# Choosing the byte offset of the weights' halves in SBUF by their use as stationary or moving operand

## The chip, the cores and the metric

The kernel runs on one core of one Trainium2 chip. The metric is the device time of one execution in microseconds (us); TensorE is called PE, VectorE DVE, ScalarE ACT, GpSimd POOL and SyncE SP, as in the profile.

## What is computed

A decoder trunk of two layers over one sequence of 256 tokens with 2048 channels, in float32. Layer 0 is attention with a forget gate (16 heads of 128), layer 1 a causal convolution module (31 taps per channel). Each has one input projection, a SiLU gate and one output projection; an RMS norm stands before each and at the end.

```python
def fox_mixer(h, w_in, b_f, w_out):          # layer 0
    q, k, v, gate, f_logit = split(h @ w_in)  # 2048 x (4*2048 + 16)
    c = cumsum(log_sigmoid(f_logit + b_f))
    s = q k^T * 128**-0.5 + c[:, None] - c[None, :]   # causal, per head
    return (softmax(s) @ v * silu(gate)) @ w_out

def conv_mixer(h, w_in, b_in, dw, dw_b, ln_g, ln_b, w_out):   # layer 1
    a, b, gate = split(h @ w_in + b_in)       # 2048 x (3*2048)
    u = conv31(a * sigmoid(b), dw) + dw_b     # causal, per channel
    return (silu(layernorm(u)) * silu(gate)) @ w_out
```

## The kernel before

**Matrices in two halves.** PE multiplies float32r numbers here. Each float32 weight or activation is therefore split into a high half (an ACT copy, `hi`, L100) and a low half (the rest, `lo`, a subtraction on DVE or POOL, L101), and each product is made of three matmuls: high by high, high by low, low by high. A weight tile is 1 MB (128 partitions by 2048 floats): SP loads it (`raw`, L112), ACT and DVE or POOL split it, PE uses it. Each of the pools `rawp`, `hip` and `lop` has three slots; ACT writes a `hi` slot when PE has finished the tile three before it.

**Two forms of projection.** `products_t` (L216) gives a transposed result. The weights' 128 columns are the stationary operand (`w[:, nt * P : ...]`), the 256 tokens of one activation tile are the moving one. One weight tile feeds 48 such matmuls. It makes q, k and the gate of layer 0, layer 0's output projection, and the whole input projection of layer 1. `products_n` (L244 to L246) gives a result by rows. There 128 tokens of the activations are stationary and 512 (in the last part 256) weight columns move. It makes v of layer 0 (`pv`) and layer 1's output projection (`po`). In the trace a matmul's row reads result<-moving,stationary.

**Where the tiles lie.** The pool `big` holds the activations: `ah`, `al` (input of layer 0, later of layer 1's first blocks), `yh`, `yl` (output of the attention), `nh`, `nl` (normed input of layer 1), `y1b` (second half of layer 1's branch output) and `xt` (halves of one late weight tile). The first half of the branch output, `ya` (in the trace `y1a`), lies in the pool `ph2`. The built kernel places all tiles of `big` and all slots of `rawp`, `hip` and `lop` at addresses that leave remainder 160 when divided by 256, since each is a multiple of 256 bytes long (16384, 8448 and 8192). Each operand is taken at a multiple of 512 bytes from its tile's start, so it keeps that remainder. `ph2` starts at 160 too, but ahead of `ya` in it lies `dwT` with 1984 bytes, 64 short of a multiple of 256, so `ya` is at remainder 96.

**Stages and order.** Layer 0 goes by four groups of heads: k, q, gate, v, and the attention of a group is put between the next group's matmuls by an agenda that counts matmul steps (`at`, `step`). PE's order is the written one throughout. From the last part of layer 0's output projection on (`all_order`), DVE, ACT and POOL run in the written order too. In layer 1 the convolution is done by DVE, one instruction for each tap and channel tile (`tap`, L824), put into PE's steps by `put` and `pump`. When a pair of channel tiles is done, ACT takes it out (`pair_end`, L876 and L877), POOL adds it to the sums for the layer norm (L880, L881, L884), and both do so in line with their share of the weights' split. After the last pair, PE adds up the rows (`column_sums`, L724, `pstat`), DVE and POOL make mean and scale (L966 to L975), and `gated` and `gated2` make `ya` and `yb` (`y1b` in the trace).

Of the kernel before, what the change touches and what calls it, by code (L numbers as in the profile page):

```python
# [8 lines left out]
F32 = mybir.dt.float32  # L9
F32R = mybir.dt.float32r  # L10
# [3 lines left out]
P = 128  # L14
D = 2048
S = 256
# [12 lines left out]
RMS_EPS = 1e-6  # L29
LN_EPS = 1e-5  # L30
LN_ROWS = 6


@with_exitstack
def tile_hybrid_trunk(
# [20 lines left out]
    const = ctx.enter_context(tc.tile_pool(name="const", bufs=1))  # L56
    big = ctx.enter_context(tc.tile_pool(name="big", bufs=1))
    rawp = ctx.enter_context(tc.tile_pool(name="rawp", bufs=3))
    hip = ctx.enter_context(tc.tile_pool(name="hip", bufs=3))
    lop = ctx.enter_context(tc.tile_pool(name="lop", bufs=3))  # L60
# [5 lines left out]
    ph = part.enter_context(tc.tile_pool(name="ph1", bufs=2))  # L66
# [5 lines left out]
    w_fin = fox_w_in[0].rearrange("(kt p) n -> p kt n", p=P)  # L72
    w_fout = fox_w_out[0].rearrange("(kt p) n -> p kt n", p=P)
    w_cin = conv_w_in[0].rearrange("(kt p) n -> p kt n", p=P)
    w_cout = conv_w_out[0].rearrange("(kt p) n -> p kt n", p=P)
# [17 lines left out]
    def load_x(c0, c1):  # L93
        nc.sync.dma_start(xn[:, :, c0:c1], xv[:, :, c0:c1])

    n_stream = [0]
    ctx.enter_context(tc.manual_schedule(engines={mybir.EngineType.PE}))

# [4 lines left out]
    def weight_tile(wv, c0, width, g, pieces=1, pool=None):  # L103

        kg = 2048 // width
        i = n_stream[0]
        n_stream[0] += 1
        raw = rawp.tile([P, 4 * NARROW], F32, tag="raw", name=f"raw{i}")[:, 0:2048]
        rv = raw.rearrange("p (k n) -> p k n", k=kg)
        kp = kg // pieces  # L110
        for q in range(pieces):
            nc.sync.dma_start(  # L112
                rv[:, q * kp : (q + 1) * kp], wv[:, g * kg + q * kp : g * kg + (q + 1) * kp, c0 : c0 + width]
            )
        return raw

    def split_tile(raw, width, lo_engs, hi=None, lo=None):

        kg = 2048 // width
        i = n_stream[0]  # L120
        n_stream[0] += 1
        if hi is None:
            hi = hip.tile([P, 2048], F32R, tag="hi", name=f"hi{i}")
            lo = lop.tile([P, 2048], F32R, tag="lo", name=f"lo{i}")
        pc = 2048 // len(lo_engs)
        for q, eng in enumerate(lo_engs):
            cs = slice(q * pc, (q + 1) * pc)
            split(hi[:, cs], lo[:, cs], raw[:, cs], eng)
        return hi.rearrange("p (k n) -> p k n", k=kg), lo.rearrange("p (k n) -> p k n", k=kg)

    def stream(wv, c0, width, lo_engs, pieces=1, ahead=False, made=(), order=None):

        kg = 2048 // width
        order = order or range(KT // kg)
        made = list(made)
        for g in range(KT // kg):
            while len(made) < (KT // kg if ahead else g + 1):
                i = len(made)
                raw = weight_tile(wv, c0, width, order[i])
                made.append(split_tile(raw, width, (lo_engs[i % len(lo_engs)],) * pieces))  # L140
            hv, lv = made[g]
            for kk in range(kg):
                yield g * kg + kk, hv[:, kk, :], lv[:, kk, :]


    feed = {"specs": [], "made": []}

    def feed_tiles(wv, c0, width, engs, order=None):

        n = KT * width // 2048  # L150
        first = len(feed["specs"])
        feed["specs"] += [(wv, c0, width, (order or range(n))[g], engs) for g in range(n)]
        return first

    def feed_make(upto):
        while len(feed["made"]) <= min(upto, len(feed["specs"]) - 1):
            wv, c0, width, g, engs = feed["specs"][len(feed["made"])]
            feed["made"].append(split_tile(weight_tile(wv, c0, width, g), width, engs))

    def fed(first, width):  # L160
        kg = 2048 // width
        for g in range(KT // kg):
            feed_make(first + g + 2)
            hv, lv = feed["made"][first + g]
            feed["made"][first + g] = None
            for kk in range(kg):
                yield g * kg + kk, hv[:, kk, :], lv[:, kk, :]
# [129 lines left out]
    with tc.manual_schedule(engines={mybir.EngineType.Activation, mybir.EngineType.DVE, mybir.EngineType.SP}):  # L297
# [40 lines left out]
        def k_split(kt):  # L338
            split_act(kt, 0, ah, al, pts[kt // 2][:, (kt % 2) * S : (kt % 2 + 1) * S])
            g, kk = kt // 4, kt % 4  # L340
            if kk == 0:
                his.append(hip.tile([P, 2048], F32R, tag="hi", name=f"hik{g}"))
                los.append(lop.tile([P, 2048], F32R, tag="lo", name=f"lok{g}"))
            cs = slice(kk * 512, (kk + 1) * 512)
            split(his[g][:, cs], los[g][:, cs], raws[g][:, cs], nc.gpsimd if kt % 2 and kt < KT - 1 else nc.vector)

# [101 lines left out]
    def gate_and_forget(c0):  # L448

        fw = ph.tile([P, KT, 2 * H], F32R, tag="v0", name="fw", bufs=1)  # L450
        ps = banks_t(512)

        pf = bank("pf")[0 : 2 * H, 0:S]
        for g in range(4):
            i = n_stream[0]
            n_stream[0] += 1
            raw = rawp.tile([P, 4 * NARROW], F32, tag="raw", name=f"raw{i}").rearrange("p (k n) -> p k n", k=4)
            nc.sync.dma_start(raw, w_fin[:, 4 * g : 4 * g + 4, c0 : c0 + NARROW])
            hi = hip.tile([P, 2048], F32R, tag="hi", name=f"hi{i}").rearrange("p (k n) -> p k n", k=4)
            lo = lop.tile([P, 2048], F32R, tag="lo", name=f"lo{i}").rearrange("p (k n) -> p k n", k=4)  # L460
            split(hi, lo, raw[:, :, 0:512], nc.vector)
            fg = fw[:, 4 * g : 4 * g + 4, :]
            split(fg[:, :, 0:H], fg[:, :, H : 2 * H], raw[:, :, 512:NARROW], nc.vector)
            for kk in range(4):
                kt = 4 * g + kk
                products_t(ps, kt, hi[:, kk, :], lo[:, kk, :], tiles(ah), tiles(al), range(4))
                if kk == 3:
                    for k in range(4 * g, kt + 1):
                        nc.tensor.matmul(pf, fw[:, k, :], ah[:, k, :], start=(k == 0), stop=False)
                        nc.tensor.matmul(pf, fw[:, k, :], al[:, k, :], start=False, stop=(k == KT - 1))  # L470
        zt = ph.tile([P, S], F32, tag="yy", name="zt")[0 : 2 * H]
        nc.vector.tensor_tensor(zt, pf, rb[0 : 2 * H, 0, :], op=ALU.mult)
        nc.vector.tensor_scalar(zt, zt, bf[0 : 2 * H], None, op0=ALU.add)
        at(2, lambda: forget_gates(zt))
        return ps
# [141 lines left out]
    for pos, hg in enumerate(ORDER):  # L617
# [38 lines left out]
            ph.tile([P, 512], dt, tag=f"v{i}", name=f"v{i}_{hg}", bufs=1) for i, dt in enumerate((F32R, F32R, F32))  # L656
        ]
        ps = [psj.tile([P, 512], F32, tag="pj", name=f"pv{hg}_{m}") for m in range(2)]
        for kt, hv, lv in stream(w_fin, 2 * D + hg * 512, 512, VE):
            for m in range(2):  # L660
                products_n(ps[m], kt, hv, lv, tiles(ah), tiles(al), m, kt == 0, kt == KT - 1)
        nc.scalar.activation(vN[0], ps[0], AF.Copy, scale=r0[:, 0:1])
# [22 lines left out]
        a_first[c0] = feed_tiles(w_cin, c0, width, GE if c0 == P else engs)  # L685
    for c in range(4):
        g_first[c] = feed_tiles(w_cin, 2 * D + c * 512, 512, GE)
    cout0 = feed_tiles(w_cout, 0, 512, VE * 2)

    def residual_add(n, b, ps):  # L690
        kp = slice(4 * n + 2 * b, 4 * n + 2 * b + 2)
# [24 lines left out]
        for b in range(2):  # L716
            residual_add(n, b, ps)

    rb1 = const.tile([P, 1, S], F32, name="rb1")

    def column_sums(ps, c0, src, last=True):

        for m in range(2):
# [21 lines left out]
    part.close()  # L745
    ph = ctx.enter_context(tc.tile_pool(name="ph2", bufs=2, reuse_waits="tile"))
    psa = ctx.enter_context(tc.tile_pool(name="psa2", bufs=3, space=bass.MemoryType.PSUM, reuse_waits="tile"))

    def kept_bank(name):

# [235 lines left out]


    HK = KT // 2
    ya = ph.tile([P, 2, HK, S], F32R, name="y1a", bufs=1)
    gts = {}  # L990

    def gated(cp):
# [99 lines left out]
        at(14 + 1.5 * i, lambda i=i: residual_rows(i // 2, i % 2))  # L1092
    for n in range(3):
        ps = [psj.tile([P, 512], F32, tag="pj", name=f"po{n}_{m}") for m in range(2)]
        for kt, hv, lv in fed(cout0, 512) if n == 0 else stream(w_cout, n * 512, 512, VE, 4):
            for m in range(2):
                products_n(ps[m], kt, hv, lv, yh, yl, m, kt == 0, kt == KT - 1)
        if n == 0:
            all_order.close()
        for m in range(2):  # L1100
            cs = slice(n * 512, (n + 1) * 512)
            nc.vector.tensor_tensor(o[:, m, cs], ps[m], o[:, m, cs], op=ALU.add)
            junk = ph.tile([P, 512], F32, tag="ev", name=f"junk{n}_{m}", bufs=4)
            nc.scalar.activation(junk, o[:, m, cs], AF.Square, accum_out=ssn[:, m, n : n + 1])
            nc.gpsimd.tensor_tensor(o[:, m, cs], o[:, m, cs], fgb[:, cs], op=ALU.mult)

    wt = []
    for g in range(4):
        raw = weight_tile(w_cout, 3 * 512, 512, g)
        if g == 0:  # L1110
            wt.append(split_tile(raw, 512, VE, xt[:, 0, :], xt[:, 1, :]))
        else:
            wt.append(split_tile(raw, 512, VE))
    for m in range(2):
        for c0, c1 in ((1536, 1792), (1792, 2048)):
            ps = psj.tile([P, 512], F32, tag="pj", name=f"po{c0}_{m}")
# [41 lines left out]
```

## Time and profile before

| | us |
|---|---|
| median of three runs | 886.54 (884.74 to 886.8) |
| the profiled execution, its time | 885.23 |
| the profiled execution, its span | 883.4 |
| PE busy | 871.9 |
| DVE busy | 569.4 |
| ACT busy | 420.6 |
| POOL busy | 363.4 |

The profile is of one execution. The span runs from the first to the last instruction; 1.8 us of the time lie around it. Matmuls overlap, so a row's mean duration is longer than the distance to the next one; the rate is read from starts in the timeline.

### The profile page before, as it was taken

What the parts mean: (1) busy time and instruction counts of PE and PEld (TensorE: products, weight loads), DVE (VectorE), ACT (ScalarE), POOL (GpSimd) and SP (SyncE); (2) the same over time, 40 slices, a digit from 0 to 9 for tenths busy, and PEclk for the clock granted to TensorE, in tenths of its full rate; (3) what the DMA queues carried; (4) which work ended last, traced back from release to release, by engine and by line L of the source; (5) the groups of instructions that cost most, each with busy time, mean ns of one, the idle gap of its engine ahead of it and who ended that gap; (6) DMA issues with size and microseconds to landing.
All of it is one profiled execution on the core that took longest, in us unless ns stands there. A gap on an engine that the chain in (4) does not pass through costs nothing.

```text
span 883.4 us, 15933 instructions
## 1 busy us (share of the span) xinstructions
PE 871.9 (99%) x6652; PEld 842.4 (95%) x6652; DVE 569.4 (64%) x1043; ACT 420.6 (48%) x558; POOL 363.4 (41%) x229
## 2 busy tenths in 40 slices
PE   9999999999999999999999999999999999999996
PEld 9999889989999899989999999999999999998896
DVE  5765456445544454446555679999999994567641
ACT  5753344345534454346544474344443455657531
POOL 4131955103410142102200068888998898521110
PEclk9999999999999999999999999999999999999998
DMA  9878988886567998965455565555555555556522
GB/s 299 222 205 189 179 155 144 165 194 174 143 185 179 173 173 153 184 190 189 135 174 178 147 191 192 191 169 193 179 179 188 162 187 189 179 191 238 180 107 96
DMA packets 99500, 157.71 MB, mean 179 GB/s; under 512 B 2676, under 2 KB 40676, under 8 KB 99300
## 3 DMA queue, kind: packets, MB, share of 16 engines
q1 hardware_dynamic: 99092, 155.63, 65.2%
q8 instruction: 52, 0.85, 0.4%
q10 hardware_dynamic: 336, 1.07, 0.3%
q14 instruction: 20, 0.16, 0.1%
HBM read 154.59 MB, written 2.10 MB: 177 GB/s over the span
## 4 chain that ended last, share of the span: by engine, by line
PE 95%; issue 1%; DMA 1%; ACT 1%; POOL 1%; DVE 0%; SPq 0%; POOLq 0%; DVEq 0%
PE pt L216 72%; PE pv L244 3%; PE pv L245 3%; PE pv L246 3%; PE po L246 3%; PE po L244 3%; PE po L245 3%; DMA rawk<-in_fox_w_in_dram 1%; PE sc L564 1%; PE ptr L593 1%; PE po L609 1%; ACT hi L100 0%; PE sc L565 0%; PE po L610 0%; PE hr L1086 0%
## 5 line engine op out<-in xcount | busy, mean ns | idle before, releaser
L100 ACT ACTIVATE hi<-raw 128x2048 fp32r<-128x2048 f32 (+2 forms) x185 | 270.6, 1486 | 303.9 <-PE pt L216 210.3
L101 DVE TENSOR_TENSOR lo<-raw,hi 128x2048 fp32r<-128x2048 f32 (+2 forms) x140 | 221.4, 1607 | 187.6 <-ACT hi L100 187.3
L101 POOL TENSOR_TENSOR lo<-raw,hi 128x2048 fp32r<-128x2048 f32 x45 | 208.1, 4641 | 42.7 <-ACT hi L100 42.7
L216 PE MATMUL pt<-ah,hi 128*128 128x256 f32 x768 | 219.6, 286 | 0.0
L216 PE MATMUL pt<-ah,lo 128*128 128x256 f32 x768 | 217.3, 283 | 0.0
L216 PE MATMUL pt<-al,hi 128*128 128x256 f32 x768 | 217.3, 283 | 0.0
L216 PE MATMUL pt<-nh,hi 128*128 128x256 f32 x704 | 199.6, 283 | 0.0
L216 PE MATMUL pt<-nh,lo 128*128 128x256 f32 x704 | 199.3, 283 | 0.0
L216 PE MATMUL pt<-nl,hi 128*128 128x256 f32 x704 | 199.2, 283 | 0.0
L824 DVE SCALAR_TENSOR_TENSOR acc<-u,dwT,acc 128x256 f32<-128x256 f32 x478 | 188.3, 472 | 0.0
L216 PEld LDWEIGHTS pt<-al,hi 128*128 128x128 f32 x768 | 147.4, 192 | 0.1
L216 PEld LDWEIGHTS pt<-ah,hi 128*128 128x128 f32 x768 | 147.3, 192 | 0.1
L216 PEld LDWEIGHTS pt<-ah,lo 128*128 128x128 f32 x768 | 147.3, 192 | 0.0
L216 PEld LDWEIGHTS pt<-nl,hi 128*128 128x128 f32 x704 | 135.1, 192 | 0.0
L216 PEld LDWEIGHTS pt<-nh,hi 128*128 128x128 f32 x704 | 135.1, 192 | 0.0
L216 PEld LDWEIGHTS pt<-nh,lo 128*128 128x128 f32 x704 | 135.1, 192 | 0.0
L216 PE MATMUL pt<-yh,hi 128*128 128x256 f32 x256 | 73.3, 286 | 0.0
L216 PE MATMUL pt<-yl,hi 128*128 128x256 f32 x256 | 72.5, 283 | 0.6 <-POOL yl L101 0.6
L216 PE MATMUL pt<-yh,lo 128*128 128x256 f32 x256 | 72.4, 283 | 0.0
L558 POOL CAST la<-ones 64x256 fp32r<-64x256 f32 x16 | 8.0, 500 | 134.9 <-PE sc L567 134.7
L244 PE MATMUL pv<-hi,ah 128*128 128x512 f32 x128 | 50.0, 390 | 0.0
L216 PEld LDWEIGHTS pt<-yl,hi 128*128 128x128 f32 x256 | 49.1, 192 | 0.8 <-POOL yl L101 0.8
(260 smaller groups left out, 1219.0 us busy)
## 6 DMA issues: line engine op xcount, KB each, us to landing
raw<-in_fox_w_in_dram SPq DMA_DIRECT2D x56, 1024.0 KB, 7.4
raw<-in_conv_w_in_dram SPq DMA_DIRECT2D x48, 1024.0 KB, 5.2
raw<-in_fox_w_out_dram SPq DMA_DIRECT2D x16, 1024.0 KB, 5.1
raw<-in_conv_w_out_dram SPq DMA_DIRECT2D x16, 1024.0 KB, 5.3
raw<-in_fox_w_in_dram SPq DMA_DIRECT2D x4, 1056.0 KB, 11.1
rawk<-in_fox_w_in_dram SPq DMA_DIRECT2D x4, 512.0 KB, 10.4
xn<-in_x_dram SPq DMA_DIRECT2D x3, 512.0 KB, 10.7
rawk<-in_fox_w_in_dram SPq DMA_DIRECT2D x4, 256.0 KB, 5.8
```

Source lines behind the costliest of these rows:

```text
L100: nc.scalar.activation(dst_hi, src, AF.Copy)
L101: lo_eng.tensor_tensor(dst_lo, src, dst_hi.bitcast(F32), op=ALU.subtract)
L216: nc.tensor.matmul(ps[nt // 2][:, (nt % 2) * S : (nt % 2 + 1) * S], w[:, nt * P : (nt + 1) * P], a(kt), start=(kt == 0 and i == 0 and nt % ...
L244: nc.tensor.matmul(ps, ah(kt)[:, ms], hv, start=first, stop=False)
L245: nc.tensor.matmul(ps, al(kt)[:, ms], hv, start=False, stop=False)
L246: nc.tensor.matmul(ps, ah(kt)[:, ms], lv, start=False, stop=last)
L558: nc.gpsimd.tensor_copy(la[0:64], ones[0:64, 0:1].broadcast_to([64, S]))
L564: nc.tensor.matmul(sc[:, 0:S], qT[q][:, j, :], kT[k][:, j, :], start=(i == 0), stop=False)
L593: nc.tensor.transpose(out=pt[:, dst * P : (dst + 1) * P], in_=p[:, srcs * P : (srcs + 1) * P], identity=ident)
L609: nc.tensor.matmul(po[:, 0:S], vN[v][:, js], pts[p], start=(i == 0), stop=False)
L824: nc.vector.scalar_tensor_tensor(acc, src, w, acc, op0=ALU.mult, op1=ALU.add)
```

## The change

Every slot of `hip` and `lop` becomes 64 floats (256 bytes) longer, and the halves begin in it at an offset. Where the weights are stationary it is 48 floats (192 bytes), which makes remainder 96. Where they move with 512 columns it is 0 (remainder 160), and where they move with 256 columns in the last part it is 16 floats (64 bytes, remainder 224). `ya` gets 16 floats of offset (remainder 160 in place of 96). To make room, `rb1` (1024 bytes) moves from the pool `const` to the start of `ph2`, which changes no remainder. `xt` stays at 160. No instruction is added, removed or put elsewhere.

```diff
+SLACK = 64
+AS_STATIONARY = 48
+AS_MOVING = 0
+AS_MOVING_256 = 16
...
+    def half_tile(pool, tag, name, off):
+        return pool.tile([P, 2048 + SLACK], F32R, tag=tag, name=name)[:, off : off + 2048]
...
-    def split_tile(raw, width, lo_engs, hi=None, lo=None):
+    def split_tile(raw, width, lo_engs, hi=None, lo=None, off=AS_STATIONARY):
...
-            hi = hip.tile([P, 2048], F32R, tag="hi", name=f"hi{i}")
-            lo = lop.tile([P, 2048], F32R, tag="lo", name=f"lo{i}")
+            hi = half_tile(hip, "hi", f"hi{i}", off)
+            lo = half_tile(lop, "lo", f"lo{i}", off)
...
-        for kt, hv, lv in stream(w_fin, 2 * D + hg * 512, 512, VE):
+        for kt, hv, lv in stream(w_fin, 2 * D + hg * 512, 512, VE, off=AS_MOVING):
...
-    cout0 = feed_tiles(w_cout, 0, 512, VE * 2)
+    cout0 = feed_tiles(w_cout, 0, 512, VE * 2, off=AS_MOVING)
...
-    rb1 = const.tile([P, 1, S], F32, name="rb1")
...
+    rb1 = ph.tile([P, 1, S], F32, name="rb1", bufs=1)
...
-    ya = ph.tile([P, 2, HK, S], F32R, name="y1a", bufs=1)
+    ya = ph.tile([P, 2 * HK * S + SLACK], F32R, name="y1a", bufs=1)[:, 16 : 16 + 2 * HK * S]
+    ya = ya.rearrange("p (i k t) -> p i k t", i=2, k=HK)
...
-        for kt, hv, lv in fed(cout0, 512) if n == 0 else stream(w_cout, n * 512, 512, VE, 4):
+        for kt, hv, lv in fed(cout0, 512) if n == 0 else stream(w_cout, n * 512, 512, VE, 4, off=AS_MOVING):
...
-            wt.append(split_tile(raw, 512, VE))
+            wt.append(split_tile(raw, 512, VE, off=AS_MOVING_256))
```

The tiles of the first k projection (`hik`, `lok`) and of the gate with the forget columns get `AS_STATIONARY` in the same way.

## Rows read from the trace of the kernel before

**Rows 1.** The page: busy time by engine; shares of the closing chain.

```profile
PE 871.9 (99%) x6652; PEld 842.4 (95%) x6652; DVE 569.4 (64%) x1043; ACT 420.6 (48%) x558; POOL 363.4 (41%) x229
...
PE 95%; issue 1%; DMA 1%; ACT 1%; POOL 1%; DVE 0%; SPq 0%; POOLq 0%; DVEq 0%
```

**Rows 2.** The chain in order of time: start us, length us, what.

```profile
545.06 197.26 PE pt L216 x1644
```

**Rows 3.** PE's groups by form: shapes, count | busy us, mean ns | idle.

```profile
L216 PE MATMUL pt<-ah,hi 128*128 128x256 f32 x768 | 219.6, 286 | 0.0
...
L216 PE MATMUL pt<-nh,hi 128*128 128x256 f32 x704 | 199.6, 283 | 0.0
...
L246 PE MATMUL po<-lo,y1a 128*128 128x512 f32 x48 | 18.8, 392 | 0.0
L246 PE MATMUL po<-lo,y1b 128*128 128x512 f32 x48 | 18.7, 390 | 0.0
...
L246 PE MATMUL po<-lo,y1b 128*128 128x256 f32 x32 | 9.0, 283 | 0.0
...
L246 PE MATMUL po<-lo,y1a 128*128 128x256 f32 x16 | 4.4, 277 | 0.0
```

**Rows 4.** Timeline of PE, first of the last four passes: start us, us.

```profile
852.54 0.28 PE L246 MATMUL po<-xt,y1a 128*128 128x256 f32 x1
...
855.01 0.28 PE L246 MATMUL po<-lo,y1a 128*128 128x256 f32 x1
...
856.08 0.28 PE L246 MATMUL po<-lo,y1b 128*128 128x256 f32 x1
...
857.88 0.28 PE L246 MATMUL po<-lo,y1b 128*128 128x256 f32 x1
```

**Rows 5.** The same timeline, second of the last four passes.

```profile
858.68 0.28 PE L246 MATMUL po<-xt,y1a 128*128 128x256 f32 x1
...
861.06 0.28 PE L246 MATMUL po<-lo,y1a 128*128 128x256 f32 x1
```

**Rows 6.** The same timeline, stationary `y1a` under 512 columns, later `y1b`.

```profile
783.70 0.39 PE L245 MATMUL po<-hi,y1a 128*128 128x512 f32 x1
...
785.99 0.39 PE L246 MATMUL po<-lo,y1a 128*128 128x512 f32 x1
...
840.98 0.39 PE L244 MATMUL po<-hi,y1b 128*128 128x512 f32 x1
...
841.66 0.39 PE L244 MATMUL po<-hi,y1b 128*128 128x512 f32 x1
```

**Rows 7.** PE's waits: us in total, times, longest us.

```profile
PE sc L566 <- POOL la L559: 2.2, 1, 2.2
```

**Rows 8.** The convolution's window: busy us (count) by engine, clock, DMA share, GB/s.

```profile
526.90:742.10 215.20, 215.15 (x1792) 214.93 (x1791) 208.53 (x542) 95.85 (x96) 189.04 (x52) 1.00 0.56 182
```

**Rows 9.** Timeline of ACT and POOL after the fifth and sixth pairs' taps.

```profile
683.97 0.51 ACT L876 ACTIVATE dall<-acc,par 128x256 f32<-128x256 f32 x1 [3.83 <-DVE acc L824]
...
694.67 18.47 POOL L101 TENSOR_TENSOR lo<-raw,hi 128x2048 fp32r<-128x2048 f32 x4
...
716.95 13.88 POOL L101 TENSOR_TENSOR lo<-raw,hi 128x2048 fp32r<-128x2048 f32 x3
```

**Rows 10.** Timeline of PE: first use of those tiles' `lo`, and the row sums.

```profile
700.64 0.28 PE L216 MATMUL pt<-nh,lo 128*128 128x256 f32 x1
...
723.68 0.28 PE L216 MATMUL pt<-nh,lo 128*128 128x256 f32 x1
...
742.53 0.58 PE L724 MATMUL pstat<-ones,accs 128*128 128x1 f32 x4
```

**Rows 11.** Timeline of DVE: its wait for the row sums.

```profile
743.15 0.16 DVE L966 TENSOR_SCALAR mean<-pstat 128x2 f32<-128x2 f32 x1 [4.58 <-PE pstat L724]
```

**Rows 12.** Timeline of POOL and PE: the gate's last weight tile.

```profile
773.18 4.63 POOL L101 TENSOR_TENSOR lo<-raw,hi 128x2048 fp32r<-128x2048 f32 x1 [6.06 <-ACT hi L100]
...
777.89 0.36 PE L216 MATMUL pt<-nh,lo 128*128 128x256 f32 x1
```

More of the change, by code (lines that the diff above doesn't have):

```diff
@@ L129, in split_tile, with stream @@
         return hi.rearrange("p (k n) -> p k n", k=kg), lo.rearrange("p (k n) -> p k n", k=kg)
-    def stream(wv, c0, width, lo_engs, pieces=1, ahead=False, made=(), order=None):
+    def stream(wv, c0, width, lo_engs, pieces=1, ahead=False, made=(), order=None, off=AS_STATIONARY):
         kg = 2048 // width
@@ L139, in stream @@
                 raw = weight_tile(wv, c0, width, order[i])
-                made.append(split_tile(raw, width, (lo_engs[i % len(lo_engs)],) * pieces))
+                made.append(split_tile(raw, width, (lo_engs[i % len(lo_engs)],) * pieces, off=off))
             hv, lv = made[g]
@@ L146, in tile_hybrid_trunk, with feed_tiles @@
     feed = {"specs": [], "made": []}
-    def feed_tiles(wv, c0, width, engs, order=None):
+    def feed_tiles(wv, c0, width, engs, order=None, off=AS_STATIONARY):
         n = KT * width // 2048
         first = len(feed["specs"])
-        feed["specs"] += [(wv, c0, width, (order or range(n))[g], engs) for g in range(n)]
+        feed["specs"] += [(wv, c0, width, (order or range(n))[g], engs, off) for g in range(n)]
         return first
@@ L156, in feed_make @@
         while len(feed["made"]) <= min(upto, len(feed["specs"]) - 1):
-            wv, c0, width, g, engs = feed["specs"][len(feed["made"])]
-            feed["made"].append(split_tile(weight_tile(wv, c0, width, g), width, engs))
+            wv, c0, width, g, engs, off = feed["specs"][len(feed["made"])]
+            feed["made"].append(split_tile(weight_tile(wv, c0, width, g), width, engs, off=off))
     def fed(first, width):
@@ L341, in k_split @@
             if kk == 0:
-                his.append(hip.tile([P, 2048], F32R, tag="hi", name=f"hik{g}"))
-                los.append(lop.tile([P, 2048], F32R, tag="lo", name=f"lok{g}"))
+                his.append(half_tile(hip, "hi", f"hik{g}", AS_STATIONARY))
+                los.append(half_tile(lop, "lo", f"lok{g}", AS_STATIONARY))
             cs = slice(kk * 512, (kk + 1) * 512)
@@ L458, in gate_and_forget @@
             nc.sync.dma_start(raw, w_fin[:, 4 * g : 4 * g + 4, c0 : c0 + NARROW])
-            hi = hip.tile([P, 2048], F32R, tag="hi", name=f"hi{i}").rearrange("p (k n) -> p k n", k=4)
-            lo = lop.tile([P, 2048], F32R, tag="lo", name=f"lo{i}").rearrange("p (k n) -> p k n", k=4)
+            hi = half_tile(hip, "hi", f"hi{i}", AS_STATIONARY).rearrange("p (k n) -> p k n", k=4)
+            lo = half_tile(lop, "lo", f"lo{i}", AS_STATIONARY).rearrange("p (k n) -> p k n", k=4)
             split(hi, lo, raw[:, :, 0:512], nc.vector)
```

## The prediction

> **What bounds the kernel now.** I read the busy times and the closing chain first. PE is busy 99% of the span and makes up 95% of the chain [rows 1]. The chain in order of time then gives the rate: one piece of it is 1644 matmuls of L216 in 197.26 us, 120.0 ns from one to the next, with no break [rows 2]. So the end is set by PE's rate, and within it by L216, the form with 256 moving columns. There are 768 of each of its three products with `ah`/`al` and 704 with `nh`/`nl` [rows 3]; by the code another 256 with `yh`/`yl` and 64 in the first k projection. That is 3 x 1792 = 5376 matmuls, or 645 us at 120.0 ns.
>
> The question is then whether 120.0 ns is the least that such a matmul takes. The kernel before holds its own experiment. In the four last passes, 256 columns move over weights at remainder 160, and the stationary operand is first `y1a` (remainder 96, 64 below the moving one), then `y1b` (160, the same). In the second pass 21 steps with `y1a` take 861.06 - 858.68 = 2.38 us, 113.3 ns each [rows 5]; the third and the fourth repeat this. In the first pass the 21 steps take 2.47 us, 117.6 ns each, and 15 steps with `y1b` take 1.80 us, 120.0 ns each [rows 4]. The mean durations show the same: 277 ns with `y1a`, 283 ns with `y1b`, and 283 to 286 in L216, whose two operands are both at 160 [rows 3]. Matmul, form, stage and moving tiles are alike, so the address of the stationary operand makes the difference.
>
> With 512 moving columns it goes the other way, a little: 10 steps with `y1a` take 2.29 us (229 ns), 3 with `y1b` 0.68 us (227 ns) [rows 6]; the means are 392 and 390 ns [rows 3].
>
> [...]
>
> **What is saved per matmul.** The three good passes save 6.7 ns each (120.0 - 113.3), the first 2.4 ns [rows 4, 5]. I can't tell what sets the first apart: ACT and DVE were at work during it and hardly in the others, but it may also be the phase in which the stream began. I take the mean of the four passes, (2.4 + 3 x 6.7) / 4 = 5.6 ns, and keep 2.4 and 6.7 as the ends.
>
> **Layer 0.** Here 2880 L216 matmuls (704 x 3 with `ah`/`al`, since 64 of each 768 belong to layer 1's first blocks, and 256 x 3 with `yh`/`yl`) save 2880 x 5.6 = 16.1 us. The feed keeps up: a tile of 48 matmuls takes 5.8 us now and 5.5 us then, and DVE, ACT and POOL have work for 64%, 48% and 41% of the span [rows 1]. The 192 matmuls of the first k projection are worth 1.1 us at most and nothing at least, since they follow the first loads; I take 0.5. Against that stands PE's one long wait, 2.2 us for POOL's part of the first head [rows 7]. POOL's forget gate runs at its own speed there, so the some 80 matmuls ahead of that wait give nothing: -0.5 us. Sum: **16.1 us**, between 6.7 and 19.9.
>
> **Layer 1, the convolution.** This stage will not give its full share. From 526.9 to 742.1 us PE is busy for 215.15 of 215.20 us, but DVE for 208.53 [rows 8], with taps that no offset makes shorter. Most of DVE's free time is one piece of 4.58 us at the end, when it waits for the row sums [rows 11]. PE at 5.6 ns less for each of some 1790 matmuls would come 10 us early and find DVE not ready. Three places hold it back; "lead" is how much earlier than now PE passes, beyond what the whole stage gains by starting earlier.
> - After the fifth pair's taps, ACT takes the pair out (it waited 3.83 us for DVE), and the weights' split and POOL's sums queue behind that. POOL then makes four `lo` tiles without a break from 694.67 on, the first of them done at 694.67 + 18.47 / 4 = 699.3, and PE reads it at 700.64 [rows 9, 10]. The lead there is at most 1.3 us.
> - After the sixth pair the same: `lo` is done at 716.95 + 13.88 / 3 = 721.6, PE reads it at 723.68 [rows 9, 10]. From the first place to here 192 matmuls bring 1.1 us, so the lead would be 2.4; the cap is 2.1.
> - At the row sums (742.53 [rows 10]) another 157 matmuls have brought 0.9 us: lead 3.0, below the 4.58 us that DVE waits there now.
>
> Ahead of the convolution, some 70 matmuls (0.4 us) count, between the output projection and the row sums that start DVE's chain. Behind the row sums there are some 340 matmuls up to the output projection, 1.9 us. Part of it goes, because the norm and gating work of DVE and ACT runs at its own speed: the gate's last `lo` tile, queued behind it, is done at 773.18 + 4.63 = 777.81 and read at 777.89 [rows 12]. I take 1.2. Sum for the stage: 0.4 + 3.0 + 1.2 = **4.6 us**, where its 2304 matmuls at the full rate would have given 13. The rest becomes short waits of PE for POOL and ACT in the gate chunks.
>
> **Output projection.** The two splits that write at a shifted address are taken at no cost: the kernel writes `y1a` at 96 and `y1b` at 160 already, inside work that PE hides. Under 512 columns `pv` stays at equal remainders, and 144 matmuls with `ya` move from 229 to 227 ns: 0.3 us. Under 256 columns `ya` over the later weight tiles stays 64 below (160 and 224), 96 matmuls with `y1b` now come 64 below: 0.5 us. The 48 with `xt`, both at 160 then, lose 0.3 us. Sum: **0.5 us**.
>
> **Total.** 16.1 + 4.6 + 0.5 = 21.2 us from the profiled 885.23 gives 864.0. That execution is 1.3 us below the median of 886.54 and inside the runs' 884.74 to 886.8, so I say **864.5**.
>
> **Rivals.**
> - **A, the weak phase.** If L216 runs as the first pass did, at 117.6 ns, perhaps because other engines are at work nearly always: layer 0 gives 6.7, the convolution and the gate some 3 (the lead is 1.3 at the first cap, and less is added), the end 0.3, in all 10 us: **875**. For it: that pass was the one with other engines busy. Against it: the steps of 229 ns under 512 columns hold with those engines at work, so their work needn't matter.
> - **B, the convolution follows.** If the three caps are not binding, because POOL and DVE have more room than I read, 5376 x 5.6 = 30 us: **855**. Against it stands DVE's 208.53 of 215.20 us.
> - **C, nothing changes.** If the difference belongs to the quiet end of the kernel or to `y1a` itself and not to the distance of 64 bytes, L216 stays at 120.0 ns: **886**. Against it: `y1b` ran at 120.0 ns in the same passes.
> - **D, slower.** Under 512 columns the distance of 64 costs 2 to 2.5 ns where equal remainders are best. If a stream whose weights are stationary behaves like that one, since the stationary tile changes between `hi` and `lo` and the moving one between `ah` and `al`, 5376 x 2.4 = 13 us are added, PE being the bound: **898**. It decides as soon as L216's step is over 120.0 ns.
>
> **How the numbers follow.** The forecast (858 to 870) has 0.63, A 0.17, B 0.07, C 0.06, D 0.07. The range reaches from the best case of the forecast to A. At 6.7 ns layer 0 gives 19.9, the row sums the full 4.6, 2.7 around them and 0.7 at the end, 27.9 us in all: 857 from the profiled time. At 2.4 ns it is 10 us, 876.5 from the median, so 877. That leaves about 0.2 outside. What a measurement here can tell from no change is about 0.3%, 2.7 us. Faster by more: forecast, A and B, 0.87. Within: C, 0.06. Slower by more: D, 0.07.
>
> **What would show it.** The step between starts of L216 at 113 to 118 ns in layer 0, and the mean duration near 277 ns; `pv` unchanged at 227 ns; `y1b` in the last passes at 113 and `xt` over `ya` back at 120. In the convolution, DVE's wait for the row sums shrinks from 4.58 us, its busy share of that window goes to 98% or more, and PE shows new waits for POOL's `lo` or DVE's `u` between 670 and 725 us. The page should show PE idle there although it is the faster engine. Wrong would be: L216 at 120 ns or more (C, D), no new waits in the gate chunks (B), or a wait long enough that the granted clock, 1.00 in this window [rows 8], falls behind it; that would cost little while DVE sets the pace.

## The result, and the profile after

The changed kernel takes 875.96 us (median of 4 runs, 875.0 to 876.41), the kernel before 886.01 us beside it (4 runs, 884.74 to 886.8): a ratio of 0.9885, 95% interval 0.9873 to 0.9897. It is faster, by 10.1 us. The forecast was 864.5, a gain of 22. The time is inside the range and within 1 us of rival A.

The profiled execution took 876.26 us (span 874.4). Line numbers of the kernel after are 6 to 10 higher: L216 is now L225. The page, busy time by engine and the closing chain (to compare with [rows 1]):

```profile
PE 861.1 (98%) x6652; PEld 831.4 (95%) x6652; DVE 569.7 (65%) x1043; ACT 420.5 (48%) x558; POOL 363.6 (42%) x229
...
PE 90%; DVE 3%; POOL 3%; issue 2%; ACT 1%; POOLq 0%; DVEq 0%
```

PE lost 10.8 us of busy time, and the other engines did what they did before. DVE and POOL, hardly in the chain before, now make up 3% of it each. The chain in order of time, start and length in us, shows the step, that is the time from one matmul's start to the next one's:

```profile
332.32 43.81 PE pt L225 x372
425.37 75.76 PE pt L225 x641
538.38 135.69 PE pt L225 x1152
692.75 41.18 PE pt L225 x346
```

The first piece has 372 matmuls in 43.81 us, 117.8 ns each; the third has 1152 in 135.69, again 117.8. (The second opens behind a wait of 0.70 us with a slower first matmul, 0.22 us to the next start; from its second start on the step is 117.8 too.) Before, it was 120.0 [rows 2]. So the saving is 2.2 ns a matmul, not 5.6. The groups by form (shapes, count | busy us, mean ns | idle) say the same:

```profile
L225 PE MATMUL pt<-ah,hi 128*128 128x256 f32 x768 | 216.8, 282 | 0.0
...
L225 PE MATMUL pt<-nh,hi 128*128 128x256 f32 x704 | 196.8, 280 | 0.0
...
L255 PE MATMUL po<-lo,y1a 128*128 128x512 f32 x48 | 18.7, 391 | 0.0
L255 PE MATMUL po<-lo,y1b 128*128 128x512 f32 x48 | 18.7, 390 | 0.0
L255 PE MATMUL po<-lo,y1b 128*128 128x256 f32 x32 | 8.9, 279 | 0.0
...
L255 PE MATMUL po<-lo,y1a 128*128 128x256 f32 x16 | 4.5, 279 | 0.0
```

L225 fell from 286 and 283 ns to 282 and 280 [rows 3], not to the 277 that `y1a` showed in the last passes before. And `y1a` itself, still 64 bytes below the moving weights, went up from 277 to 279. The timeline of PE has both steps of the answer in it, first in a stretch of the gate and then in the first of the last four passes:

```profile
769.46 0.28 PE L225 MATMUL pt<-nh,hi 128*128 128x256 f32 x1
...
774.45 0.28 PE L225 MATMUL pt<-nh,lo 128*128 128x256 f32 x1
...
846.01 0.28 PE L253 MATMUL po<-hi,y1b 128*128 128x256 f32 x1
...
848.72 0.28 PE L255 MATMUL po<-lo,y1b 128*128 128x256 f32 x1
```

The 44 steps of the first stretch take 4.99 us, 113.4 ns each; the 23 steps with `y1b`, now 64 bytes below too, take 2.71 us, 117.8 each. I followed the starts of all 66 stretches of 256-column matmuls in this trace (62 of L225, 4 of the last passes); a stretch is a run of them that nothing interrupts. Wherever the stationary operand is 64 bytes below, the step is one of two, 113.3 or 117.8 ns. A stretch has one from its first few matmuls and keeps it to its end, up to some 1250 matmuls long. But 113.3 is rare: 4 stretches, 110 of some 5600 matmuls. In the kernel before, three passes of four with `y1a` had it [rows 5].

### The profile page after: what moved, and what is told of

It reads as the page before. It is cut to its first block, busy times and chain, and to the rows that moved or that the text cites. A ratio compares the mean times of both kernels' runs of the same rounds, so it can differ in the third digit from the quotient of the medians.

```text
span 874.4 us, 15933 instructions
## 1 busy us (share of the span) xinstructions
PE 861.1 (98%) x6652; PEld 831.4 (95%) x6652; DVE 569.7 (65%) x1043; ACT 420.5 (48%) x558; POOL 363.6 (42%) x229
## 4 chain that ended last, share of the span: by engine, by line
PE 90%; DVE 3%; POOL 3%; issue 2%; ACT 1%; POOLq 0%; DVEq 0%
PE pt L225 66%; PE pv L253 3%; PE pv L255 3%; PE pv L254 3%; PE po L253 3%; PE po L255 3%; PE po L254 3%; POOL lo L110 2%; DVE acc L833 1%; ACT hi L109 1%; PE sc L573 1%; PE warm L335 1%; PE ptr L602 1%; PE po L618 1%; PE tp L280 0%
## 5 line engine op out<-in xcount | busy, mean ns | idle before, releaser
L225 PE MATMUL pt<-ah,hi 128*128 128x256 f32 x768 | 216.8, 282 | 0.0
L225 PE MATMUL pt<-ah,lo 128*128 128x256 f32 x768 | 214.8, 280 | 0.0
L225 PE MATMUL pt<-al,hi 128*128 128x256 f32 x768 | 214.3, 279 | 0.0
L225 PE MATMUL pt<-nh,lo 128*128 128x256 f32 x704 | 196.7, 279 | 1.4 <-POOL lo L110 1.2
L225 PE MATMUL pt<-nl,hi 128*128 128x256 f32 x704 | 197.0, 280 | 0.0
L225 PE MATMUL pt<-nh,hi 128*128 128x256 f32 x704 | 196.8, 280 | 0.0
L225 PEld LDWEIGHTS pt<-al,hi 128*128 128x128 f32 x768 | 144.4, 188 | 0.1
L225 PEld LDWEIGHTS pt<-ah,lo 128*128 128x128 f32 x768 | 144.1, 188 | 0.0
L225 PEld LDWEIGHTS pt<-ah,hi 128*128 128x128 f32 x768 | 143.9, 187 | 0.1
L225 PEld LDWEIGHTS pt<-nh,lo 128*128 128x128 f32 x704 | 131.7, 187 | 2.0 <-POOL lo L110 1.6
L225 PEld LDWEIGHTS pt<-nh,hi 128*128 128x128 f32 x704 | 132.3, 188 | 0.1
L225 PEld LDWEIGHTS pt<-nl,hi 128*128 128x128 f32 x704 | 132.2, 188 | 0.0
L225 PE MATMUL pt<-yh,hi 128*128 128x256 f32 x256 | 72.5, 283 | 0.0
L225 PE MATMUL pt<-yl,hi 128*128 128x256 f32 x256 | 71.5, 279 | 0.7 <-POOL yl L110 0.7
L225 PE MATMUL pt<-yh,lo 128*128 128x256 f32 x256 | 71.5, 279 | 0.0
L254 PE MATMUL pv<-hi,al 128*128 128x512 f32 x128 | 49.8, 389 | 0.0
## 6 DMA issues: line engine op xcount, KB each, us to landing
rawk<-in_fox_w_in_dram SPq DMA_DIRECT2D x4, 512.0 KB, 10.8
```

Source lines behind the costliest of these rows:

```text
L225: nc.tensor.matmul(ps[nt // 2][:, (nt % 2) * S : (nt % 2 + 1) * S], w[:, nt * P : (nt + 1) * P], a(kt), start=(kt == 0 and i == 0 and nt % ...
L254: nc.tensor.matmul(ps, al(kt)[:, ms], hv, start=False, stop=False)
```

## The experiments

The theory was that the address decides, through two steps of which the entry into a stretch picks one. Its rivals were that the changed layout in general made the gain, and that the work of other engines holds the step at 117.8 (the reason offered for rival A). For each kernel I give the median and the kernel before beside it.

**Only the offset.** The changed kernel with one constant altered, 0, 128 or 64 bytes above instead of 64 below:

```diff
-AS_STATIONARY = 48
+AS_STATIONARY = 0     # e1; 32 in e2 (128 bytes away), 16 in e3 (64 bytes above)
```

> The changed kernel with AS_STATIONARY = 0: the weights' halves are back at equal remainders where they are stationary; the longer slots, the move of rb1, ya's offset and the last part's offset stay. Theory: the whole gain comes from the step of products_t, so it is back at 120.0 ns and the time at 884 to 887 us. Rival (layout: the gain comes from the moved pools or from the last stage): 875 to 878 us.

> The changed kernel with AS_STATIONARY = 32, that is 128 bytes below (or above) the activations' remainder. If only equal remainders collide, the step of products_t is 117.7 ns as at 64 below, and the time 875 to 877 us. If the distance matters in finer steps, the step is another one, and the time moves by 2.3 us in layer 0 for each ns of the 2 to 3 us that the convolution lets through.

> The changed kernel with AS_STATIONARY = 16, that is 64 bytes above the activations' remainder. If only equal remainders collide: 117.7 ns, 875 to 877 us. If the sign matters (the stationary operand is read ahead of the moving one), it is slower than 64 below: up to 120 ns and 886 us.

Beside 886.97 for the kernel before, e1 took 885.9 us (ratio 0.9995, interval 0.9985 to 1.0006), e2 880.7 (0.9931, 0.9915 to 0.9948) and e3 868.33 (0.9794, 0.9776 to 0.9812). The same piece of the chain, first in e1, then in e2, then in e3, with the convolution's first stretch behind it for e3:

```profile
336.77 44.64 PE pt L225 x372
```

```profile
335.87 44.15 PE pt L225 x372
```

```profile
328.04 42.18 PE pt L225 x372
...
419.10 72.94 PE pt L225 x641
...
529.28 135.69 PE pt L225 x1152
```

That is 120.0, 118.7 and 113.4 ns a matmul, where the changed kernel has 117.8. With equal addresses the whole gain is gone, longer slots, moved `rb1` and all: it belongs to the offset. And 64 bytes above gains 18.6 us where 64 below gained 10.1; I had expected it to be equal or slower. (In the kernel before, the weights of one L216 matmul start to load at 250.00 us and the matmul itself starts at 250.12, so the stationary operand is 0.12 us ahead; that this would make 64 above the slower side was my guess, and e3 shows the opposite.) Even there the step is one of the two: the piece of 1152 has 117.8, but 45 of L225's 62 stretches have 113.3, against 4 in the changed kernel. The four runs of e3 lie in two pairs, near 867.1 and near 869.6 us. The one shown here belongs to the first pair. That a long stretch took the other step in the second pair would fit, but is not shown.

**The offset by itself.** A kernel of its own that has only PE's streams, 24 matmuls of L225's form each, with the weights 0 to 240 bytes above the activations:

```diff
+    for off in range(0, 64, 4):                      # floats
+        8 x (three transposes; stream(off))
+        4 x (wait for an ACT instruction; stream(off))
+        4 x (three matmuls of 512 columns; stream(off))
```

> A kernel of its own that leaves the whole model out (its output is zeros): streams of 24 matmuls in the form of products_t (128 stationary columns, 256 moving ones, hi-hi, hi-lo, lo-hi) with all activations at one remainder and the weights' halves at that remainder plus 0, 16, 32, ... 240 bytes; 16 streams for each offset, 8 entered after three transposes, 4 after a wait for ACT, 4 after three matmuls with 512 columns. Other engines rest meanwhile. Theory P (phase): a stream settles in one of two steps at its entry and keeps it, whatever the other engines do. Then at 192 bytes some streams run at 113.3 ns and others at 117.7, though nothing else works. Theory E (engines; the reason given for rival A): 117.7 ns comes of other engines at work, so here all streams at 192 bytes run at 113.3 ns. Both: 120.0 ns at 0 bytes. Open for both: whether another offset is always at 113.3 ns or below.

The mean step of each stream, worked out from its starts, without its first five steps:

| weights above activations, bytes | step, ns |
|---|---|
| 0 | 119.7 to 120.1 |
| 16, 32 | 118.0 to 118.6 |
| 48 | 117.7 to 118.3 (two streams 123.3) |
| 64 | 113.3 to 113.4, all 16 streams |
| 80, 96, 112 | 117.3 to 120.4 |
| 128 | 118.4 to 120.0 |
| 144, 160 | 119.6 to 120.1 |
| 176 | 117.9 to 118.2 |
| 192 (the change: 64 below) | 113.3 in 6 streams, 117.8 in 10 |
| 208, 224 | 116.4 to 117.8 |
| 240 | 117.2 or 119.9 to 120.1 |

Four streams as the chain has them: offset 0, offset 64, and two of offset 192, one right behind the other:

```profile
16.20 2.88 PE s L97 x24
...
229.76 2.74 PE s L97 x24
...
668.87 2.73 PE s L97 x24
671.93 2.83 PE s L97 x24
```

With nothing else running, a stream 64 below takes 2.73 or 2.83 us, by chance as it seems, after the same three transposes.

**The other engines.** The same streams, 64 below, 64 above and equal in turn, entered after one to five transposes; 56 rounds with PE alone, then 56 while ACT, DVE and POOL split tiles:

```diff
+    rounds()                                          # PE alone
+    270 x activation(hi2, raw); 250 x DVE and 80 x POOL tensor_tensor(lo, raw, gate)
+    rounds()                                          # the same, beside them
```

> A kernel of its own that computes nothing of the model: streams of 24 matmuls with 256 moving columns, each entered after one to five transposes, in turn with the weights' halves 64 bytes below, 64 above and (every fourth time) at the activations' remainder; 56 rounds with PE alone, then 56 rounds while ACT, VectorE and POOL split tiles without a break. Theory (the step is set when the stream is entered): both halves show the same mixture, 64 below between 113.3 and 117.7 ns in some streams each, 64 above at 113.3 nearly always, equal at 120.0; no stream changes its step within itself when the other engines work. Rival (other engines' work makes the step 117.7): with PE alone all streams 64 below at 113.3, with the engines busy all at 117.7 or above, and the equal ones above 120.0.

The window without them and the window with them; busy us and counts of PE, its weight load, DVE, ACT and POOL, then granted clock, DMA share and GB/s:

```profile
20.00:400.00 380.00, 380.00 (x3273) 380.00 (x3272) 0.00 (x0) 0.00 (x0) 0.00 (x0) 1.00 0.00 1
420.00:790.00 370.00, 370.00 (x3188) 370.00 (x3187) 368.07 (x57) 364.00 (x190) 365.61 (x57) 1.00 0.00 1
```

Of 56 streams 64 below, 6 had 113.3 with PE alone and 6 with ACT, DVE and POOL busy; of 56 streams 64 above, 30 and 32, where I had expected nearly all; the 14 equal ones had 120.0 both times. The other engines' work made no difference to these counts. What did was how the stream was entered. Both windows together, 64 below gave 113.3 in 12 of 22 streams after three transposes and in 0 of 90 after one, two, four or five. 64 above gave it in 6 of 24, 16 of 22, 13 of 22, 5 of 22 and 22 of 22 after one to five.

**The entry, in the kernel itself.** The changed kernel with three (r3) or four (r4) transposes of a constant ahead of every 48 of L225's matmuls in the convolution, and the variant with 64 above with five (r5):

```diff
+        if again["n"] > 48:
+            for j in range(3):   # 4 in r4; 5 in r5, with AS_STATIONARY = 16
+                nc.tensor.transpose(out=<unused half of pm's bank>, in_=ones[:, 0:P], identity=ident)
```

> The changed kernel (64 bytes below) with three transposes of a constant, written to an unused half of the bank of the channels' mean, ahead of every 48 of L225's matmuls between the mean shift and the gate's rows: some 35 more entries into that stream, about 0.3 us each, so 884 to 888 us. The trace decides: theory (the entry sets the step), in my own kernel 12 of 22 streams entered after three transposes took 113.3 ns, so of these some 35 stretches about half (8 to 27) at 113.3 and the rest at 117.7, each constant within itself. Rival (in this kernel something else keeps the step at 117.7, the other engines or the transfers): none at 113.3.

> The same with four transposes in each place. Theory, with the count of transposes deciding as it did in my own kernel (0 of 22 after four): all or nearly all stretches at 117.7, at most 3 at 113.3. Rival (an entry of any kind gives a chance of half): about half at 113.3.

> The variant with the halves 64 bytes above, with five transposes in each of these places. Theory, by my own kernel (22 of 22 after five): nearly all stretches at 113.3, at least 30 of some 35. Rival (this kernel's entries are not those of my own kernel): a mixture, or 117.7 as in the long stretch of the variant without them.

The times, one run each, 891.76, 886.92 and 880.2 us beside 885.06, carry the added work; one transpose also waits 2.5 us for DVE to have read that bank. The chain's pieces of 48, in r3, then r4, then r5 (L225 is their L234):

```profile
579.88 5.66 PE pt L234 x48
585.87 5.66 PE pt L234 x48
```

```profile
575.90 5.45 PE pt L234 x48
581.79 5.45 PE pt L234 x48
587.67 5.66 PE pt L234 x48
593.77 5.45 PE pt L234 x48
```

```profile
579.97 5.46 PE pt L234 x48
585.97 5.46 PE pt L234 x48
```

In r4, 22 of the 35 stretches have 113.3 and 13 have 117.8, in a pattern of two short and one long that repeats through the whole convolution. In r5 all 35 have 113.3. In r3 one has it, which began right after that wait, where the granted clock was 0.57 over 4 us; the other 34 are at 117.8. (In r4 the stretch behind that wait began at a granted clock of 0.57 too, and has 117.8.) So the entry picks the step in this kernel too, with its DMA, ACT, DVE and POOL at work. The part of my expectation that carried the counts over from my own kernel was wrong: three transposes gave 1 of 35 here, and four gave nearly two thirds. So the number alone isn't what decides; what it acts on is not shown.

**The convolution's own pace.** The kernel before (t1), after (t2) and with 64 above (t3), with 16 of the 31 taps left out of DVE's work:

```diff
+        if first is None and t > 14:
+            return                                    # the place in the order stays empty
```

> The kernel before, with 15 of the convolution's 31 taps computed on VectorE and the other 16 left out (their places in the written order stay empty). PE has the same 6652 matmuls. Theory (PE's rate sets the end of the kernel before): hardly shorter than 886, between 884 and 887, although VectorE loses about 16 x 16 x 0.39 = 100 us of work. Rival (VectorE's taps set the pace of the convolution already): more than 3 us shorter. It is the base for the next two.

> The changed kernel (64 bytes below) with the same taps left out. Theory (a saving of 2.3 ns for each of 5376 matmuls, of which the convolution's chain on VectorE, ACT and POOL swallowed about 2 us): with the chain eased the gain over the kernel before with the same taps left out is 11.5 to 12.5 us, and PE no longer waits for POOL's lo after the fifth pair. Rival (POOL's own splits hold that place, whatever the taps): the gain stays at 9.5 to 10.3 us.

> The variant with the halves 64 bytes above, with the same taps left out. Theory: its waits of 1.7 us ahead of the mean shift, 1.5 and 0.6 us in the gate chunks and 0.9 us at the gate's last tile go, and the gain over the kernel before with the same taps left out rises from 18 to about 22 us (21 to 24). Rival (the waits belong to POOL's own splits): 17.5 to 18.5 us.

Measured: t1 885.88 us beside 886.78 for the kernel before (0.9993, interval 0.9984 to 1.0002), t2 873.87 (0.9854, 0.984 to 0.9867), t3 856.24 (0.9664, 0.9645 to 0.9684). So DVE's 99 us less are worth nothing to the kernel before and 2 us to the one after. With 64 above the time is 12 us shorter, but there the stretches took other steps as well, as the rows show. The gain over t1 is 12.0 and 29.6 us where all taps left 10.1 and 18.6. Rows of the chain in t2, then in t3:

```profile
426.08 72.92 PE pt L225 x641
...
535.39 193.63 PE pt L225 x1644
```

```profile
417.35 75.77 PE pt L225 x641
...
528.25 186.34 PE pt L225 x1644
```

Without the taps the 1644 matmuls run in one piece again, as in [rows 2]. t2 has the changed kernel's step of 117.8 in it, so its 2 us are what the taps held back: between the mean shift and the row sums PE's lead on its base (how much earlier it passes the same matmul) grows by 3.6 us in t2 and by 1.7 in the changed kernel, and t2 has no wait of PE for POOL's `lo` left. In the execution of t3 shown here this entry happened to give 113.3 for all 1644 (186.34 us), which I hadn't counted on: 1644 x 4.4 ns = 7.2 us, about as much as its 29.6 exceed my 22. What the taps alone are worth with 64 above is therefore not shown. The pieces of 641 are telling as well. Up to there t2 is the same program as the changed kernel, and t3 the same as e3; yet t2 has the short form (72.92) where the changed kernel has the long (75.76), and t3 the long where e3 has the short (72.94). One program can take either.

**The version with both.** 64 bytes above in L225, and in the last four passes the moving weights placed so that `y1a` and `y1b` are 64 above them:

```diff
-AS_MOVING_256 = 16
+AS_MOVING_256 = 48      # and AS_STATIONARY = 16
```

> 64 bytes above in L225, and the weights that move in the last four passes placed so that the stationary y1a and y1b are 64 bytes above them too (for all but the first weight tile, which lies elsewhere). Theory: 144 matmuls of the last passes come from about 117.7 to 113.3 ns, 0.6 us, so 867.7 where the variant with 64 above ran in 868.3. Rival (in the last passes another thing sets the step): 868.3, no difference. The two differ by less than the runs scatter, so the steps in the trace decide.

866.84 us beside 886.78 (0.9778, interval 0.9765 to 0.9791). It beats both kernels; against e3, whose interval overlaps, no more can be said. `y1b` in the last passes, and its longest piece in layer 0:

```profile
L255 PE MATMUL po<-lo,y1b 128*128 128x256 f32 x32 | 8.8, 276 | 0.0
```

```profile
417.53 75.77 PE pt L225 x641
```

At 276 ns instead of 279 the passes took the short step. Here the piece of 641 has the long form, worth 641 x 4.4 ns = 2.8 us.

## Why the prediction was off

**The bound, and that the address matters: right.** PE's rate set the end (t1), and L225's step fell with no other change (e1).

**What is saved per matmul: the step that failed.** I took the mean of four passes, 5.6 ns; measured are 2.2, at the low end (2.4) that I named. The mean was one over two fixed steps and four entries, and all four entries were of one kind: each pass of [rows 4, 5] begins behind the residual's matmul against the identity, four rows of the trace, here ahead of the second pass in the kernel before.

```profile
858.00 0.61 PE L1049 MATMUL po<-ident,hT 128*128 128x128 f32 x4
```

There 113.3 came in three passes of four. L225 is entered in other ways, mostly after matmuls of attention and after waits, and got 113.3 in 4 of 62 stretches. I had named the phase in which the stream began as a possible cause, and then used a rate as if each matmul drew anew. In the 66 stretches that I followed it is drawn once per stretch, so three long stretches (some 1250, 640 and 370 matmuls) hold two fifths of the outcome.

**Rival A: right in size, wrong in reason.** It gave 875 with 117.6 ns and put it to other engines at work. m2 (6 of 56 with and without them) and r4 and r5 refute that; the entry does it. That its number came out is luck as far as its reason goes.

**Layer 0: 16.1 us foretold.** Matched matmul by matmul, PE is 6.5 us ahead of the kernel before at its 500.5 us. That is close to 2880 x 2.2 = 6.3 us, so only the size of the step was off.

**The convolution: the caps were right.** Where PE stood at the first of them, and what POOL, DVE and the window (as in [rows 8]) say:

```profile
692.75 0.38 PE L225 MATMUL pt<-nh,lo 128*128 128x256 f32 x1 [1.20 <-POOL lo L110]
...
688.05 13.92 POOL L110 TENSOR_TENSOR lo<-raw,hi 128x2048 fp32r<-128x2048 f32 x3
...
734.74 0.16 DVE L975 TENSOR_SCALAR mean<-pstat 128x2 f32<-128x2 f32 x1 [2.86 <-PE pstat L731]
...
519.90:733.70 213.80, 211.95 (x1792) 211.22 (x1792) 208.84 (x543) 94.50 (x96) 189.20 (x52) 1.00 0.57 184
```

At the tile read at 700.64 before [rows 10], PE now waits 1.20 us for POOL, whose first of three `lo` tiles is done at 688.05 + 13.92 / 3 = 692.7. The lead falls from 9.2 to 7.9 us there. Counted from the mean shift, where it was 6.7, that leaves 1.2; the cap foretold was 1.3. With 64 above it is 17.1 - 15.8 = 1.3 us. PE had the step of 117.8 there too, so this shows that the cap stays when the whole stage comes 9 us earlier, and not what a faster step would meet. DVE's wait for the row sums shrank from 4.58 [rows 11] to 2.86 us, by 1.7 instead of 3.0, since the smaller step reaches only that far. DVE's busy share over the same 1792 matmuls went from 96.9 to 97.7%, close to the 98 foretold. From layer 0's end to the output projection, all this brought 8.9 - 6.5 = 2.4 us, against 4.6.

One wait I had not foreseen: at the mean shift, which opens DVE's chain, PE waits for the first channel's sum.

```profile
537.71 0.67 PE L866 MATMUL pm<-dall,ones 128*128 128x256 f32 x2 [0.62 <-DVE dall L857]
```

It costs 0.6 us here, and 1.7 with 64 above.

**Output projection: 0.5 us foretold, 0.1 measured (the lead goes from 8.9 to 9.0).** Under 512 columns the two halves came together as foretold (391 and 390 ns). But `y1a`'s passes lost the short step they had before (277 to 279 ns), which took back what `y1b` gained.

**Rivals B to D.** B fell twice: the rate wasn't there, and the convolution doesn't follow (a lead of 1.7 us where 3.6 came without the taps). C fell with e1. D's step above 120.0 occurred in no stretch that I followed in the kernel after.

The distance of the two operands modulo 256 bytes is worth 17.6 us here (885.9 in e1, 868.33 in e3). That it counts modulo 256 shows in t3: the slots of `hip` and `lop` are 8448 bytes long, 33 x 256, and the piece of 1644 matmuls goes through them at one step (186.34 us, 113.3 ns each). At 256 columns no stretch here was under 113.3 ns a matmul; under 512 columns [rows 6] show 227 to 229 ns.

What stays open: what in an entry picks the step. It differs between runs whose programs are the same up to that stretch (the pieces of 641), repeats in a pattern of three in r4, and depends on what stood ahead of the stream in a way that two kernels don't share.

## What to carry to other kernels

Where PE is the bound and its matmuls come back to back in this form (float32r, 128 stationary and 256 moving columns), place the stationary operand 64 bytes above the moving one, modulo 256, and look at the step from start to start: it went from 120.0 to between 113.3 and 117.8 ns here. Under 512 columns 64 below cost 2 ns a matmul [rows 6], and 64 above was not tried. When a rate from a trace comes in two sizes, ask for what span it is drawn before you average it; four short stretches entered in one way say little about some sixty entered in others. And look for the chain that takes over: in the convolution half of what PE saved ended in waits for POOL and DVE (a lead of 1.7 us where 3.6 came without the taps).

## What was unexpected

The distance of 64 bytes isn't symmetric: above it gave 113.3 ns in all 16 streams of m1 and in 62 of 112 of m2, below it in 6 of 16 and 12 of 112. Only at these two distances, of sixteen tried, did 113.3 occur. At 48 and 32 bytes below, 31 of 32 streams lay at 116.4 to 117.0, under the 117.8 that the changed kernel mostly has; these distances were not tried in the kernel. The step is kept by stretches of over a thousand matmuls (the piece of 1152 at 117.8 ns in the changed kernel, that of 1644 at 113.3 in t3) with DMA, ACT, DVE and POOL at work beside them (in the changed kernel's convolution a DMA share of 0.57, and ACT busy for 94.50, DVE for 208.84 and POOL for 189.20 of 213.80 us).

In r3, after PE had waited 2.5 us for DVE in the added transposes, the granted clock was 0.57 in the next 4 us, and 21 matmuls ran in them. In r4 the same followed a wait of 2.6 us, with 19 matmuls in 3.76 us; in r5 the clock stayed at 1.00 behind a wait of 2.5 us, with 35 matmuls in 3.94 us. What makes the difference is not shown. The windows, in r3, r4 and r5:

```profile
554.00:558.00 4.00, 4.00 (x21) 4.00 (x22) 4.00 (x11) 0.40 (x1) 4.00 (x1) 0.57 0.67 234
...
549.50:553.50 4.00, 3.76 (x19) 3.76 (x20) 4.00 (x11) 0.42 (x1) 4.00 (x1) 0.57 0.67 230
...
543.10:547.10 4.00, 3.94 (x35) 3.94 (x36) 4.00 (x12) 0.42 (x1) 4.00 (x1) 1.00 0.66 227
```

In the changed kernel, a wait of 1.20 us in the convolution left the clock at 1.00 (the window of 1792 matmuls above).
